# The ends of two feed-forwards: weight splits, residual updates and transposes put in a stated order

## The chip, the cores and the metric

The kernel runs on one core of one Trainium2 chip, in one launch. The metric is the device time of the program in microseconds (us). The engines are named as in the profile: PE is TensorE (PEld its weight loads), DVE is VectorE, ACT is ScalarE, POOL is GpSimd and SP is SyncE, which issues most DMAs. Each engine works through its own list of instructions strictly in the order of that list; an instruction that waits holds up all that stand behind it.

## The reference, cut to what matters

One decoder layer on 512 tokens of width 1024, in float32:

```python
h = x + 0.5 * swiglu(rmsnorm(x, ffn1_norm), ffn1_w_gate, ffn1_w_up, ffn1_w_down)     # width 2816
n = rmsnorm(h, mix_norm)
z = n @ w_in                          # queries, keys, values and gates of two kinds of heads
h = h + concat(attention(z), gla(z)) @ w_out
h = h + 0.5 * swiglu(rmsnorm(h, ffn2_norm), ffn2_w_gate, ffn2_w_up, ffn2_w_down)
gate = sigmoid(rmsnorm(h, ple_gate_norm) @ ple_w_gate)      # 1024 x 1024
emb = rmsnorm(p @ ple_w_proj, ple_norm)                     # 256 -> 1024
h = h + gate * emb

def swiglu(x, w_gate, w_up, w_down):
    return (silu(x @ w_gate) * (x @ w_up)) @ w_down
def rmsnorm(x, g):
    return x * rsqrt(mean(x * x) + 1e-6) * g
```

## The kernel before

**Tiles and products.** The 512 tokens are four tiles of 128. The running sum `h` is four tiles of 128 tokens by 1024 columns. Every large product is made from three PE products: both factors are split into a high part (`hi`, rounded to the PE's float32r) and a low part (`lo`, what is left), and hi·hi, hi·lo and lo·hi are added in one PSUM bank (`mm3`). So each weight tile is loaded by a DMA (`wraw`), cast by ACT to `whi` (line 140) and subtracted by DVE to `wlo` (line 141). `Weights` does this in a fixed order of units: `load` issues the DMA into one of two raw buffers of 1 MB, `split` casts and subtracts into a ring of five slots, and `get(key, ahead)` splits up to a key and some units further.

**The end of a feed-forward.** The last 256 of the 2816 inner columns are handled apart. For each token tile t, `pd(t, q)` makes the last down products for two inner chunks q, into two PSUM banks; `update(t)` adds half of them to `h[t]` (DVE, line 391). The next step needs the norm of `h[t]` turned so that columns lie on partitions: `squares` (ACT, line 307, two halves with their sums), `factor` (a small DVE sum, line 312, and the power -1/2 on POOL, line 299), `scaled` (DVE, line 316), and `turned`, which is `norm_transpose`: eight PE transposes (line 202) into two banks, each bank copied out by an ACT cast to `nhi` (line 292) and a DVE subtraction to `nlo` (line 293). The function `last_tiles` writes out in what order these steps are recorded for the four tiles; `in_order` ties each step behind the last instruction of PE, ACT and DVE recorded so far. A scheduler then puts the instructions of each engine in a list, and may move what isn't tied.

**What follows the two ends.** After the first feed-forward come the products `pe` (p times `ple_w_proj`; four tiles, each 12 PE products and an ACT copy to `eo`), with the last two tiles' transposes after `pe` of tile 1, and then the input projections of the mixing part, first `kvr` (keys, values, ranks). The `pe` products stand in PSUM banks in which the last two `pd` lay, so that they wait for the updates of `h`. After the second feed-forward comes the last gate `pg`: for each half of the columns and each tile, 24 products (`pgt`), a sigmoid on ACT (line 1065), and on DVE the product with `emb` (line 1066) and the sum with `h` (line 1067), then a DMA out. Its weights are four units of 1 MB before.

Of the kernel before, what the change touches and what calls it, by code (L numbers as in the profile page):

```python
# [152 lines left out]
def hymba_kernel(tc, A, out):  # L153
# [50 lines left out]
    def on_pe(f, *args):  # L204

        with tc.issue_after(last_pe[0]):
            return f(*args)
# [76 lines left out]
    for c0 in (0, 512):  # L284
        for k0 in (0, 4):
            W.add_rows("pg", A["ple_w_gate"], k0, 4, c0, 512)

# [35 lines left out]

    def last_tiles(pd, update, gain, nT, name, third=(), fourth=()):

# [12 lines left out]
        def turned(t):  # L338
            norm_transpose(t, sq[t][0], nT, name, (psA, psG))

        in_order((pd, 0, 0), (pd, 1, 0), (pd, 0, 1), (update, 0), (squares, 0), (pd, 1, 1), (update, 1), (factor, 0),
                 (squares, 1), (pd, 2, 0), (pd, 2, 1), *third, (scaled, 0), (update, 2), (factor, 1), (squares, 2),
                 (pd, 3, 0), (pd, 3, 1), (scaled, 1), *fourth, (turned, 0), (update, 3), (factor, 2), (squares, 3),
                 (scaled, 2), (turned, 1), (factor, 3), (scaled, 3))
        return turned
# [211 lines left out]
    with tc.tile_pool(name="ffn1p", bufs=1, reuse_waits="tile") as fp:  # L557
# [4 lines left out]
        turned = []  # L562

        def finish1(pd, update):
            turned.append(last_tiles(pd, update, lambda: gm, nTm, "mx", (), [(keep, 0), (keep, 1), (keep, 2)]))
            keep(3)

        def keep(t):
            nc.sync.dma_start(out=h_d[t], in_=h[t])
# [41 lines left out]
    for t in range(0, NT, 2):  # L611
        eo = mp.tile([P, 8, 256], F32, name=f"eo{t}", tag="e", bufs=2).rearrange("p (t a) c -> p t (a c)", t=2)
        for i in range(2):
# [4 lines left out]
            nc.sync.dma_start(out=emb_d[t + i], in_=eo[:, i])  # L618
            if t + i in (1, 2):
                turned[0](t + i + 1)  # L620

# [376 lines left out]
    with tc.tile_pool(name="ffn2p", bufs=1, reuse_waits="tile") as fp:  # L998
# [38 lines left out]
        nT3 = norm_pair(np_, "pg")  # L1037
        def split_gates():
            W.get(("pg", 0, 0), 0)

        def finish2(pd, update):
            turned[:] = [last_tiles(pd, update, lambda: g3[0], nT3, "pg", [(split_gates,)])]

# [3 lines left out]
    with tc.tile_pool(name="outp", bufs=1, reuse_waits="tile") as op:  # L1047
# [6 lines left out]
        for c0 in (0, 512):  # L1054
            tiles = [W.get(("pg", c0, k)) for k in (0, 2, 4, 6)]
            for t in range(NT):
                if c0 == 0 and t in (1, 2):
                    turned[0](t + 1)
                parts = ((0, 256), (256, 512)) if c0 and t == NT - 1 else ((0, 512),)
                for a, b in parts:  # L1060
                    sl = slice(c0 + a, c0 + b)
                    ps = psA(f"pgt{c0}_{t}_{a}")[:, :b - a]
                    gemm_ts(ps, nT3, t, [(wh[:, :, a:b], wl[:, :, a:b]) for wh, wl in tiles])
                    sg = op.tile([P, 512], F32, name=f"sgm{c0}_{t}_{a}", tag="sgm", bufs=3)[:, :b - a]
# [63 lines left out]
```

## Time and profile before

| | |
|---|---|
| three runs, median (lowest to highest) | 1008.62 us (1008.01 to 1010.85) |
| the profiled execution: its time, and its span from first to last instruction | 1008.22 us, 1006.5 us |
| PE busy | 971.2 us, 96% of the span |
| DVE, ACT, POOL busy | 64%, 39%, 4% |
| mean granted clock of PE | 0.989 of full speed |

The span is what the trace covers; the time of the execution is 1.7 us more. All positions below are microseconds from the start of the span. The first feed-forward ends at about 364 us and the second at about 948 us. In a row of a timeline the first number is the start, the second how long the row's instructions took from the first's start to the last's end, `x16` how many instructions are merged in it, and a bracket at its end says how long the engine stood idle before it and what released it. Matmuls are pipelined: one 128x512 product is shown with 0.39 us, while the next one starts 0.227 us later.

### The profile page before, as it was taken

The page shows a single profiled execution, that of the slowest core. Times are in us where ns is not written, and L with a number is a line of the kernel's source. Part 1 is how long each engine was busy: PE and PEld are TensorE (multiplying, and loading weights), DVE is VectorE, ACT ScalarE, POOL GpSimd, SP SyncE. Part 2 cuts the span into 40 slices and gives each one's busy share as a digit, 9 for nine tenths or more (in the row PEclk, how much of TensorE's full clock was granted, in tenths as well). Part 3 has the DMA queues.
Part 4 walks back from the last instruction along what each step waited for, and adds up shares of the span by engine and source line. Part 5 has one row for each costly group of instructions (what it writes and reads, how often), then busy time and mean ns, then how long its engine had stood idle before and what let it go on. Part 6 is the DMA issues. An engine that isn't in the chain of part 4 may idle for free.

```text
span 1006.5 us, 12373 instructions
## 1 busy us (share of the span) xinstructions
PE 971.2 (96%) x5090; PEld 807.4 (80%) x5090; DVE 645.0 (64%) x811; ACT 394.5 (39%) x569; POOL 43.7 (4%) x55
## 2 busy tenths in 40 slices
PE   5999999999999989998998999999999999999898
PEld 5988888888888879876766789888888888888687
DVE  6567667576675764775766364766677675757652
ACT  5443333333333245585455243333344333332441
POOL 4000000000000010200002010000000000000010
PEclk9999999999999999999998999999999999999999
DMA  8715133141330255220213246142252523303231
GB/s 290 250 47 168 41 126 125 46 167 40 126 105 1 88 186 184 88 85 1 58 50 98 84 163 242 42 168 84 96 205 75 169 83 106 124 1 104 74 126 53
DMA packets 74235, 109.91 MB, mean 109 GB/s; under 512 B 5937, under 2 KB 55234, under 8 KB 74178
## 3 DMA queue, kind: packets, MB, share of 16 engines
q1 hardware_dynamic: 72450, 102.82, 30.4%
q0 software_dynamic: 1728, 6.29, 1.8%
q8 instruction: 40, 0.66, 0.2%
q14 instruction: 17, 0.14, 0.0%
HBM read 100.72 MB, written 8.39 MB: 108 GB/s over the span
## 4 chain that ended last, share of the span: by engine, by line
PE 88%; DVE 6%; ACT 2%; DMA 2%; issue 1%; POOL 0%; SPq 0%; ACTq 0%; POOLq 0%; DVEq 0%
PE pg L199 24%; PE pu L199 24%; PE pd L199 20%; PE pgt L199 5%; PE wo L199 4%; PE aq L199 2%; PE pe L199 1%; PE kvr L199 1%; PE gqk L199 1%; PE gv L199 1%; PE gog L199 1%; DVE mx L724 1%; DMA wraw<-in_w_out_dram 1%; DVE wlo L141 1%; DVE e L722 1%
## 5 line engine op out<-in xcount | busy, mean ns | idle before, releaser
L140 ACT CAST whi<-wraw 128x1024 fp32r<-128x1024 f32 (+1 forms) x126 | 129.9, 1039 | 187.4 <-PE pd L199 136.3
L141 DVE TENSOR_TENSOR wlo<-wraw,whi 128x1024 fp32r<-128x1024 f32 (+1 forms) x124 | 149.9, 1215 | 56.0 <-ACT whi L140 53.7
L199 PE MATMUL pg<-nlo_f,whi 128*128 128x512 f32 (+1 forms) x384 | 143.0, 373 | 0.0
L199 PE MATMUL pg<-nhi_f,whi 128*128 128x512 f32 (+1 forms) x384 | 142.6, 373 | 0.2 <-ACT nhi_f L292 0.2
L199 PE MATMUL pu<-nhi_f,wlo 128*128 128x512 f32 (+1 forms) x384 | 142.6, 372 | 0.0
L199 PE MATMUL pg<-nhi_f,wlo 128*128 128x512 f32 (+1 forms) x384 | 142.6, 372 | 0.0
L199 PE MATMUL pu<-nlo_f,whi 128*128 128x512 f32 (+1 forms) x384 | 142.6, 372 | 0.0
L199 PE MATMUL pu<-nhi_f,whi 128*128 128x512 f32 (+1 forms) x384 | 142.4, 372 | 0.0
L199 PE MATMUL pd<-whi,ahi 128*128 128x512 f32 x312 | 121.4, 389 | 0.0
L199 PE MATMUL pd<-wlo,ahi 128*128 128x512 f32 x312 | 121.4, 389 | 0.0
L199 PE MATMUL pd<-whi,alo 128*128 128x512 f32 x312 | 120.6, 389 | 0.0
L391 DVE SCALAR_TENSOR_TENSOR h<-pd,h 128x512 f32<-128x512 f32 x116 | 76.5, 686 | 29.5 <-PE pd L199 29.5
L199 PEld LDWEIGHTS pg<-nhi_f,whi 128*128 128x128 f32 x384 | 72.3, 189 | 13.2 <-ACT nhi_f L292 0.7
L199 PEld LDWEIGHTS pg<-nlo_f,whi 128*128 128x128 f32 x384 | 72.6, 189 | 12.9 <-DVE nlo_f L293 0.6
L199 PEld LDWEIGHTS pg<-nhi_f,wlo 128*128 128x128 f32 x384 | 72.5, 189 | 12.5
L199 PEld LDWEIGHTS pu<-nhi_f,wlo 128*128 128x128 f32 x384 | 72.3, 188 | 12.5
L199 PEld LDWEIGHTS pu<-nhi_f,whi 128*128 128x128 f32 x384 | 72.2, 188 | 12.5
L199 PEld LDWEIGHTS pu<-nlo_f,whi 128*128 128x128 f32 x384 | 72.4, 188 | 12.3
L140 ACT CAST whi<-draw 128x1024 fp32r<-128x1024 f32 x35 | 36.8, 1053 | 96.9 <-PE pu L199 50.9
L431 DVE TENSOR_TENSOR cb<-pu,sg 128x512 f32<-128x512 f32 x44 | 30.3, 690 | 69.2 <-PE pu L199 69.2
L140 ACT CAST whi<-wpr 128x1024 fp32r<-128x1024 f32 x35 | 36.9, 1053 | 96.2 <-PE pu L199 58.2
L199 PEld LDWEIGHTS pd<-whi,ahi 128*128 128x128 f32 x312 | 58.6, 188 | 12.2
(243 smaller groups left out, 1466.5 us busy)
## 6 DMA issues: line engine op xcount, KB each, us to landing
wraw<-in_ffn_w_gate_dram SPq DMA_DIRECT2D x22, 1024.0 KB, 5.0
wraw<-in_ffn_w_up_dram SPq DMA_DIRECT2D x22, 1024.0 KB, 5.0
wpr<-in_ffn_w_down_dram SPq DMA_DIRECT2D x10, 1024.0 KB, 5.6
draw<-in_ffn_w_down_dram SPq DMA_DIRECT2D x10, 1024.0 KB, 5.2
wraw<-in_w_in_dram SPq DMA_DIRECT2D x8, 1024.0 KB, 4.9
wraw<-in_ple_w_gate_dram SPq DMA_DIRECT2D x4, 1024.0 KB, 4.8
h<-in_x_dram SPq DMA_DIRECT2D x4, 512.0 KB, 7.0
wraw<-in_ffn_w_down_dram SPq DMA_DIRECT2D x4, 512.0 KB, 3.4
```

What stands on the lines that cost most here:

```text
L140: nc.scalar.copy(hi, v)
L141: (nc.gpsimd if u < 2 and i else nc.vector).tensor_tensor(lo, v, hi.bitcast(F32), op=ALU.subtract)
L199: last_pe[0] = nc.tensor.matmul(o, lhsT=l, rhs=r, start=start, stop=stop_, **kw).ins
L391: nc.vector.scalar_tensor_tensor(hs, x, 0.5, hs, ALU.mult, ALU.add)
L431: nc.vector.tensor_mul(cb[:, half].rearrange("p a c -> p (a c)"), pu, sg)
L722: nc.vector.tensor_add(half, sc[:, :, :, :nk], amask[:, 256 - nk:].unsqueeze(1).unsqueeze(1).broadcast_to([P, 2, 2, nk]))
L724: nc.vector.reduce_max(mxt.rearrange("p (g a) -> p g a", g=2)[:, :, 2 * a:2 * a + 2], half, AX.X)
```

## The change

Three things are written anew. First, the order of the steps in `last_tiles`: the common part now ends with the last `pd`, and each feed-forward gives a list of `places` for the rest. Second, the first two of the `pg` weights for the first half of the columns are loaded and split as two units of 512 KB instead of one of 1 MB, the first of them before the last down products, the next two between the steps of the second end; and the first `kvr` unit is split at a stated place of the first end. Third, the last two tiles' transposes: after the first end the code has them behind `pe` of tiles 0 and 1 instead of 1 and 2 (on PE's list they stand behind `pe` of tile 1 in both kernels; new there is that the first twelve products of `kvr` tile 0 follow them, ahead of `pe` of tile 2), and in the gate they stand in the middle of the 24 products of tiles 1 and 2 instead of ahead of them.

```diff
     for c0 in (0, 512):
-        for k0 in (0, 4):
-            W.add_rows("pg", A["ple_w_gate"], k0, 4, c0, 512)
+        for k0, nk in ((0, 2), (2, 2), (4, 4)) if c0 == 0 else ((0, 4), (4, 4)):
+            W.add_rows("pg", A["ple_w_gate"], k0, nk, c0, 512)
...
-    def last_tiles(pd, update, gain, nT, name, third=(), fourth=()):
+    def last_tiles(pd, update, gain, nT, name, places):
...
-        in_order((pd, 0, 0), (pd, 1, 0), (pd, 0, 1), (update, 0), (squares, 0), (pd, 1, 1), (update, 1), (factor, 0),
-                 (squares, 1), (pd, 2, 0), (pd, 2, 1), *third, (scaled, 0), (update, 2), (factor, 1), (squares, 2),
-                 (pd, 3, 0), (pd, 3, 1), (scaled, 1), *fourth, (turned, 0), (update, 3), (factor, 2), (squares, 3),
-                 (scaled, 2), (turned, 1), (factor, 3), (scaled, 3))
+        named = {"pd": pd, "update": update, "squares": squares, "factor": factor, "scaled": scaled, "turned": turned}
+        in_order((pd, 0, 0), (pd, 1, 0), (pd, 0, 1), (update, 0), (squares, 0), (pd, 1, 1), (update, 1), (squares, 1),
+                 (factor, 0), (pd, 2, 0), (pd, 2, 1), (scaled, 0), (factor, 1), (update, 2), (scaled, 1),
+                 (pd, 3, 0), (pd, 3, 1), *((named.get(f, f), *args) for f, *args in places))
         return turned
...
-            turned.append(last_tiles(pd, update, lambda: gm, nTm, "mx", (), [(keep, 0), (keep, 1), (keep, 2)]))
-            keep(3)
+            turned.append(last_tiles(pd, update, lambda: gm, nTm, "mx", [
+                ("update", 3), ("turned", 0), ("squares", 2), ("factor", 2), ("turned", 1), ("squares", 3),
+                (keep, 0), (keep, 1), ("scaled", 2), ("factor", 3), (keep, 2), (lambda: W.get(("kvr", 0, 0), 0),),
+                ("scaled", 3), (keep, 3)]))
...
-            if t + i in (1, 2):
-                turned[0](t + i + 1)
+            if t + i < 2:
+                turned[0](t + i + 2)
...
-        def split_gates():
-            W.get(("pg", 0, 0), 0)
+        def split_gates(k):
+            W.get(("pg", 0, k), 0)

         def finish2(pd, update):
-            turned[:] = [last_tiles(pd, update, lambda: g3[0], nT3, "pg", [(split_gates,)])]
+            split_gates(0)
+            turned[:] = [last_tiles(pd, update, lambda: g3[0], nT3, "pg", [
+                ("squares", 2), ("turned", 0), ("factor", 2), (split_gates, 2), (split_gates, 4), ("turned", 1),
+                ("scaled", 2), ("update", 3), ("squares", 3), ("factor", 3), ("scaled", 3)])]
...
-                if c0 == 0 and t in (1, 2):
-                    turned[0](t + 1)
...
-                    gemm_ts(ps, nT3, t, [(wh[:, :, a:b], wl[:, :, a:b]) for wh, wl in tiles])
+                    wt = [(wh[:, :, a:b], wl[:, :, a:b]) for wh, wl in tiles]
+                    if c0 == 0:
+                        on_pe(gemm_ts, ps, nT3, t, wt[:2], False)
+                        if t in (1, 2):
+                            on_pe(turned[0], t + 1)
+                        on_pe(gemm_ts, ps, nT3, t, wt[2:], True, 4)
+                    else:
+                        gemm_ts(ps, nT3, t, wt)
```

What stands on the engines can differ from what the code's order says, since the scheduler fills in. Three places follow, each as it was and as it is. In the names, the number at the end is the buffer's; `h_92`, `h_93` and `h_94` are tiles 1, 2 and 3 of `h` in the first part.

DVE at the end of the first feed-forward, before: the update of tile 3 is the third step from the end.

```order
L391 SCALAR_TENSOR_TENSOR h_93<-pd_0_2_2606,h_93 128x512
L391 SCALAR_TENSOR_TENSOR h_93<-pd_1_2_2610,h_93 128x512
L312 SCALAR_TENSOR_TENSOR ms_mx_2623<-ss_mx_2603 128x1
L316 SCALAR_TENSOR_TENSOR nrm_mx_2602<-h_92,rs_mx_2625,gain_mix_norm 128x1024
L141 TENSOR_TENSOR wlo_0_2804<-wraw_2800,whi_0_2803 128x544
L141 TENSOR_TENSOR wlo_1_2808<-wraw_2800,whi_1_2807 128x544
L293 TENSOR_TENSOR nlo_mix<-ntr_mx_0_2649,nhi_mix 128x4x128
L293 TENSOR_TENSOR nlo_mix<-ntr_mx_1_2656,nhi_mix 128x4x128
L391 SCALAR_TENSOR_TENSOR h_94<-pd_0_3_2631,h_94 128x512
L391 SCALAR_TENSOR_TENSOR h_94<-pd_1_3_2635,h_94 128x512
```

The same place after:

```order
L312 SCALAR_TENSOR_TENSOR ms_mx_2621<-ss_mx_2599 128x1
L391 SCALAR_TENSOR_TENSOR h_93<-pd_0_2_2606,h_93 128x512
L391 SCALAR_TENSOR_TENSOR h_93<-pd_1_2_2610,h_93 128x512
L316 SCALAR_TENSOR_TENSOR nrm_mx_2598<-h_92,rs_mx_2623,gain_mix_norm 128x1024
L391 SCALAR_TENSOR_TENSOR h_94<-pd_0_3_2628,h_94 128x512
L391 SCALAR_TENSOR_TENSOR h_94<-pd_1_3_2632,h_94 128x512
L293 TENSOR_TENSOR nlo_mix<-ntr_mx_0_2644,nhi_mix 128x4x128
L293 TENSOR_TENSOR nlo_mix<-ntr_mx_1_2651,nhi_mix 128x4x128
```

The update of tile 3 stands directly behind the scaling of tile 1; the two `kvr` weight splits and the first `nlo` copies, which stood ahead of it, stand behind it (the splits now between the small sum and the scaling of tile 3).

DVE at the end of the second feed-forward, before: `nrm_pg_7039` and `nrm_pg_7055` are the scaled tiles 0 and 1, which the first transposes read.

```order
L312 SCALAR_TENSOR_TENSOR ms_pg_7051<-ss_pg_7040 128x1
L141 TENSOR_TENSOR wlo_0_7076<-wraw_7073,whi_0_7075 128x1024
L141 TENSOR_TENSOR wlo_1_7080<-wraw_7073,whi_1_7079 128x1024
L316 SCALAR_TENSOR_TENSOR nrm_pg_7039<-h_0_4388,rs_pg_7053,gain_ple_gate_norm 128x1024
L391 SCALAR_TENSOR_TENSOR h_2_4390<-pd_0_2_7059,h_2_4390 128x512
L391 SCALAR_TENSOR_TENSOR h_2_4390<-pd_1_2_7063,h_2_4390 128x512
L312 SCALAR_TENSOR_TENSOR ms_pg_7086<-ss_pg_7056 128x1
L141 TENSOR_TENSOR wlo_0_7168<-wraw_7165,whi_0_7167 128x1024
L141 TENSOR_TENSOR wlo_1_7172<-wraw_7165,whi_1_7171 128x1024
L316 SCALAR_TENSOR_TENSOR nrm_pg_7055<-h_1_4389,rs_pg_7088,gain_ple_gate_norm 128x1024
```

The same place after, where `nrm_pg_7045` and `nrm_pg_7057` are those two tiles:

```order
L312 SCALAR_TENSOR_TENSOR ms_pg_7061<-ss_pg_7046 128x1
L316 SCALAR_TENSOR_TENSOR nrm_pg_7045<-h_0_4388,rs_pg_7063,gain_ple_gate_norm 128x1024
L312 SCALAR_TENSOR_TENSOR ms_pg_7080<-ss_pg_7058 128x1
L391 SCALAR_TENSOR_TENSOR h_2_4390<-pd_0_2_7065,h_2_4390 128x512
L391 SCALAR_TENSOR_TENSOR h_2_4390<-pd_1_2_7069,h_2_4390 128x512
L316 SCALAR_TENSOR_TENSOR nrm_pg_7057<-h_1_4389,rs_pg_7082,gain_ple_gate_norm 128x1024
L293 TENSOR_TENSOR nlo_pg<-ntr_pg_0_7105,nhi_pg 128x4x128
L293 TENSOR_TENSOR nlo_pg<-ntr_pg_1_7112,nhi_pg 128x4x128
L312 SCALAR_TENSOR_TENSOR ms_pg_7119<-ss_pg_7102 128x1
L141 TENSOR_TENSOR wlo_0_7126<-wraw_7123,whi_0_7125 128x1024
L141 TENSOR_TENSOR wlo_0_7132<-wraw_7129,whi_0_7131 128x1024
L141 TENSOR_TENSOR wlo_1_7136<-wraw_7129,whi_1_7135 128x1024
```

Four weight splits stood between the small sum of tile 0 and the scaling of tile 1. Now none does: one stands far ahead, just before the first addition to `U_0` behind the last product of chunks 16 to 19, and three behind the first `nlo` copies.

PE in the gate, before: `pgt_0_0_7195` and `pgt_1_0` are tiles 0 and 1 of the first half of the columns, `nrm_pg_7090` and `nrm_pg_7129` the scaled tiles 2 and 3.

```order
L199 MATMUL pgt_0_0_7195<-whi_1_7171,nlo_pg 128x512
L202 MATMUL ntr_pg_1_7232<-idn,nrm_pg_7090 128x128 x4
L202 MATMUL ntr_pg_0_7225<-idn,nrm_pg_7090 128x128 x4
L202 MATMUL ntr_pg_1_7276<-idn,nrm_pg_7129 128x128 x4
L199 MATMUL pgt_1_0_7239<-whi_0_7075,nhi_pg 128x512
```

The same tiles after, where `nrm_pg_7101` is the scaled tile 2:

```order
L199 MATMUL pgt_1_0_7227<-wlo_0_7126,nhi_pg 128x512
L199 MATMUL pgt_1_0_7227<-whi_0_7125,nlo_pg 128x512
L202 MATMUL ntr_pg_0_7240<-idn,nrm_pg_7101 128x128 x4
L202 MATMUL ntr_pg_1_7247<-idn,nrm_pg_7101 128x128 x4
L199 MATMUL pgt_1_0_7227<-whi_0_7131,nhi_pg 128x512
```

The gate of tile 1 follows that of tile 0 at once; the transposes of tile 2 stand behind its twelfth product, and those of tile 3 behind the twelfth and the eighteenth of tile 2.

## Rows read from the trace of the kernel before

**Rows 1.** Who waited for whom, PE: total us, times, longest us.

```profile
PE ntr_pg L202 <- ACT whi L140: 3.7, 1, 3.7
PE pe L199 <- DVE h L391: 2.5, 1, 2.5
```

**Rows 2.** Chain that ended last, 350 to 400 us: start, us, what.

```profile
369.14 7.38 PE pe L199 x24
...
378.27 5.46 PE pe L199 x24
383.72 11.98 PE kvr L199 x96
```

**Rows 3.** Timeline of PE, at the two ends and at 575 us.

```profile
364.47 2.16 PE L202 MATMUL ntr_mx<-idn,nrm_mx 128*128 128x128 f32 x16
...
575.03 0.50 PE L199 MATMUL wo<-wlo,nhi_mo 128*128 128x512 f32 x1 [1.69 <-DVE wlo L141]
...
948.94 1.06 PE L202 MATMUL ntr_pg<-idn,nrm_pg 128*128 128x128 f32 x8 [1.04 <-DVE nrm_pg L316]
953.67 1.57 PE L202 MATMUL ntr_pg<-idn,nrm_pg 128*128 128x128 f32 x8 [3.67 <-ACT whi L140]
...
969.28 0.50 PE L199 MATMUL pgt<-whi,nhi_pg 128*128 128x512 f32 x1 [0.25 <-ACT sgm L1065]
```

**Rows 4.** Timeline of DVE, end of the first feed-forward.

```profile
362.06 1.28 DVE L391 SCALAR_TENSOR_TENSOR h<-pd,h 128x512 f32<-128x512 f32 x2
...
364.13 1.29 DVE L316 SCALAR_TENSOR_TENSOR nrm_mx<-h,rs_mx,gain_mix_norm 128x1024 f32<-128x1024 f32 x1 [0.73 <-POOL rs_mx L299]
365.34 1.35 DVE L141 TENSOR_TENSOR wlo<-wraw,whi 128x544 fp32r<-128x544 f32 x2
366.61 1.28 DVE L293 TENSOR_TENSOR nlo_mix<-ntr_mx,nhi_mix 128x512 fp32r<-128x512 f32 x2
367.81 1.28 DVE L391 SCALAR_TENSOR_TENSOR h<-pd,h 128x512 f32<-128x512 f32 x2
```

**Rows 5.** Timeline of ACT, end of the first feed-forward.

```profile
362.77 0.63 ACT L307 ACTIVATE nrm_mx<-h 128x512 f32<-128x512 f32 x1 [1.84 <-DVE h L391]
...
365.27 1.07 ACT L292 CAST nhi_mix<-ntr_mx 128x512 fp32r<-128x512 f32 x2
```

**Rows 6.** Stretches: us; busy of PE, PEld, DVE, ACT, POOL; PE clock; DMA.

```profile
371.00:372.00 1.00, 1.00 (x4) 0.80 (x3) 1.00 (x3) 0.00 (x0) 0.00 (x0) 0.50 1.05 428
...
576.00:577.00 1.00, 1.00 (x6) 0.79 (x5) 1.00 (x2) 0.00 (x0) 0.00 (x0) 1.00 0.00 0
```

**Rows 7.** Timeline of DVE, end of the second feed-forward.

```profile
945.24 2.36 DVE L141 TENSOR_TENSOR wlo<-wraw,whi 128x1024 fp32r<-128x1024 f32 x2 [1.77 <-ACT whi L140]
947.52 1.28 DVE L316 SCALAR_TENSOR_TENSOR nrm_pg<-h,rs_pg,gain_ple_gate_norm 128x1024 f32<-128x1024 f32 x1
...
949.98 2.35 DVE L141 TENSOR_TENSOR wlo<-wraw,whi 128x1024 fp32r<-128x1024 f32 x2
952.25 1.28 DVE L316 SCALAR_TENSOR_TENSOR nrm_pg<-h,rs_pg,gain_ple_gate_norm 128x1024 f32<-128x1024 f32 x1
```

**Rows 8.** Chain that ended last, 945 to 975 us.

```profile
955.25 6.55 PE pgt L199 x24
```

**Rows 9.** Timeline of POOL, end of the second feed-forward.

```profile
943.62 0.55 POOL L299 TENSOR_TENSOR rs_pg<-ms_pg,nhalf 128x1 f32<-128x1 f32 x1 [180.74 <-DVE ms_pg L312]
950.21 1.40 POOL L299 TENSOR_TENSOR rs_pg<-ms_pg,nhalf 128x1 f32<-128x1 f32 x1 [6.04 <-DVE ms_pg L312]
```

**Rows 10.** Timelines of SP, ACT and DVE, 915 to 927 us.

```profile
917.65 5.17 SPq L104 DMA_DIRECT2D wraw<-in_ple_w_gate_dram  x2
...
920.11 1.05 ACT L140 CAST whi<-wraw 128x1024 fp32r<-128x1024 f32 x1 [3.75 <-PE pd L199]
...
925.28 0.69 DVE L412 TENSOR_TENSOR U<-U,pd 128x512 f32<-128x512 f32 x1 [1.66 <-PE pd L199]
```

**Rows 11.** Weight loads (`wraw`) between 905 and 980 us: time to landing.

```profile
DMA to landing us min/median/max: 3.4/4.8/5.8
```

## The prediction, made before the result was known

> **What bounds the kernel now.** I read the busy shares first: PE works 96% of the span, so what can be won is PE's idle time and the time in which it runs at the lower clock. The list of PE's waits comes next. It names two places which the change touches: 2.5 us before the first `pe`, put down to DVE's update of `h`, and 3.7 us before a transpose in the gate, put down to an ACT cast [rows 1]; PE's own timeline adds 1.04 us before the transposes of tile 0 [rows 3]. Then I looked at what the engine named did just before.
>
> At the first end PE's 16 transposes run from 364.47 to 366.63 [rows 3], and `pe` starts at 369.14 [rows 2]. DVE shows why: the update of tile 3 ends at 369.09, since the scaling of tile 1, two `kvr` splits (1.35 us) and two `nlo` copies (1.28 us) stand ahead of it [rows 4], although its products were done when the transposes began. The wait has a second price. In the stretch 371 to 372 the clock is 0.50, the level of 1.2 GHz [rows 6], and the 24 products of `pe` tiles 0 and 1 take 7.38 us where the next 24 take 5.46 [rows 2].
>
> At the second end the scaling of tile 0 starts at 947.52 behind two splits (2.36 us), and that of tile 1 at 952.25 behind two more (2.35 us) [rows 7]. PE's transposes start at 948.94 and 953.67 [rows 3], each right after the scaling that it reads. So the 3.7 us are DVE's too; the ACT cast merely ended at the same moment. The first 24 gate products then take 6.55 us [rows 8] instead of 5.46.
>
> **The change part by part. First end.** The update of tile 3 now follows the scaling of tile 1. The small sum of tile 1 stands ahead of the update of tile 2, so that update runs about 0.15 us later than 362.06 and ends at 363.4. The power of tile 1 was there 0.88 us after its sum's start (0.15 sum, 0.73 wait [rows 4]), now at 363.0, hidden by the update. The scaling runs 363.4 to 364.7, 0.7 earlier than 364.13. The last `pd` ends where the transposes begin, so the update of tile 3 runs from about 364.7 to 366.0. The banks of `pe` are free 0.6 us before PE has finished its transposes at 366.63. The wait of 2.51 goes, and with it the slow clock, 7.38 − 5.46 = 1.92. Together 4.43.
>
> What is late next? PE would end the 24 `pe` at 372.1 and transposes of tile 2 at 373.1; tile 3 must be scaled by then. ACT casts the first `nhi` pair 365.3 to 366.3 (0.8 us after the transposes start as now, 1.07 long [rows 3, 5]), then squares of tile 2 (two halves of 0.63) to 367.5, the second `nhi` pair to 368.6, squares of tile 3 to 369.8, two `kvr` casts to 371.1. DVE follows: `nlo` pair of tile 0 366.0 to 367.2, `nlo` of tile 1 to 369.3, scaling of tile 2 to 370.6, sum of tile 3 to 370.7, two `kvr` splits to 372.0, scaling of tile 3 then to 373.3, if the power of 0.88 us is hidden under the splits. Beside a split POOL's power took 1.40 us, without one 0.55 [rows 9], so it may come 0.85 later, and the scaling ends between 373.3 and 373.7. PE waits 0.2 to 0.7 us there; I take 0.5. The trace agrees with the Trainium skill, "SBUF — State Buffer", section "SBUF: two separate sides": whichever of DVE and GpSimd takes the shared port pair first has it for a whole instruction. By that rule the upper end counts, and the gain would be 0.2 us less.
>
> Nothing else at this end costs PE time. The first 12 of the 96 `kvr` products (11.98 us in all [rows 2], so 1.5) only change places with `pe` of tiles 2 and 3, and cover the copy of `eo`, which ACT now does behind `nhi` of tile 2. The second load of the queries' weights leaves SP when `kvr`'s split frees its buffer, 372 instead of 366.7, but its cast comes after 382, and loads landed within 5.8 us [rows 11]. The four writes of `h` stand ahead of it on SP and are ready by 366. First end: 4.43 − 0.5 = 3.9. Bounds: 2.5 with the clock still falling and 0.5 more in stalls, 4.4 with no new wait.
>
> **Second end.** The first split moves far ahead, in front of an addition to `U` on DVE. The cast of the unit before it starts at 920.11, when the fourth of seven groups of products has freed a ring slot [rows 10]; the fifth group, 12 products of 0.227, frees the next near 922.8. Its load leaves SP at 917.65 [rows 10] and is half as long as before. ACT stands idle from 921.2, so the cast ends near 923.9 and the split near 925.1, ahead of the addition at 925.28. It costs nothing; behind it some 8 us of additions wait, with 3 us to spare before the last `pd` need their factors.
>
> With no split ahead, tile 0's power is there at 944.2 (943.62 + 0.55 [rows 9]) and its scaling done at 945.5, before the last `pd` end at 947.9 (948.94 − 1.04). The update of tile 2 runs to 946.8, the scaling of tile 1 to 948.0. PE turns both tiles without a gap from 947.9, in 2.16 us as at the first end [rows 3], to 950.05. The first gate product needs `nlo` of tile 0. ACT's squares of tile 2 are done at 948.1, its `nhi` pair runs 948.7 to 949.7, DVE's pair ends at 950.5, its first half at 949.9: no wait. Six products (1.36 us) use the split made early. The seventh and eighth need the second one: ACT casts it 949.7 to 950.75 (1.05 [rows 10]), DVE splits it by 952.0, while PE asks at 951.4, so PE waits 0.6. The third and fourth follow at 1.2 us each (half of 2.35 [rows 7]) and PE takes 1.36 for six products, so these are in time. The 24 products end at about 956.0 where they now end at 961.8 (955.25 + 6.55 [rows 8]), 5.8 earlier.
>
> From there tile 1's 24 products need its `nlo` (955.3) and free bank; the transposes of tile 2 come after twelve, at 958.7, and its scaling ends at 956.7. Those of tile 3 are asked for at about 965.1. Its scaling waits for a chain: the sigmoid of tile 0 (956.1 to 956.7), a cast for the next half, two squares (to 959.3), sum, power, `nlo` of tile 2: done near 961.9, three microseconds early. The 0.25 us for the sigmoid [rows 3] goes: the third tile's product takes the bank that tile 2's transposes left. Against this I set 0.3 us for `nlo` of tile 3, which now stands behind two products with `emb` on DVE. Second end: 5.8. Bounds: 3.5, if two bank waits (0.6 covered by transposes plus 0.25 each) and another 0.6 in the weights return; 6.5, if there is no wait at all (13.9 us from 947.9 to 961.8 against 2.16 + 5.46, plus 0.25).
>
> The one load more costs SP half a microsecond in an idle time. The mixing part between keeps its order; its waits hang on PE's own earlier results and move with it.
>
> **The sum.** 1008.22 (span 1006.5 and 1.7 around it) − 3.9 − 5.8 = 998.5. The profiled execution lies 0.4 below the median 1008.62, so I predict 998.9 for the median.
>
> **Rivals.** (a) *The gate gives a part back.* After the scaling of tile 1 DVE has `nlo`, three splits, `nlo` and a scaling without a pause, and ACT its casts in between; if one comes late, PE works in pieces. For it: DVE is the last engine at every step there. Against: PE's demand is slower than DVE's supply. Price: a pause as long as that before `pe` would bring a slow spell like its own, 1.9 us [rows 2]: 1000.8. That short waits alone bring the lower clock the rows don't show: after 1.69 us of idleness at 573 [rows 3] the stretch 576 to 577 has clock 1.00, 2.4 GHz [rows 6]. The Trainium skill says otherwise, in "TensorE: Matmul & The Clock Gate", section "A second HAM failure mode": frequent small idle times between groups of matmuls can make the clock oscillate. By that rule the price of (a) would fall due although no wait is long.
>
> (b) *Only the gate counts.* The mixing part has stretches where PE waits for ACT and DVE; if their work didn't start earlier by the 3.9 us, the first end would be given back: 1008.6 − 5.8 = 1002.8. Against: what DVE and ACT do there starts from products of PE, and nothing is bound to a fixed time.
>
> (c) *The change doesn't act.* If `pe` and the transposes wait for something else than the named steps, all stays: 1008.6. Against: three starts that follow an end on DVE within 0.25 us.
>
> (d) *Slower.* ACT's list has the cast of the next half's first weights between the first sigmoid and the squares of tile 3. This load leaves SP only when the second split frees its buffer, at 952.0. While it is out, ACT stands, and behind it the squares, the scaling and the transposes of tile 3, amid tile 2's products on PE. It is due at 956.7 (median 4.8 [rows 11]), and there are 3 us in hand; from 960 on every microsecond counts in full, and from a landing at 970 the kernel is slower than before. With a landing at 973, 1012. Against: no load here took over 5.8 us.
>
> **How the numbers follow.** Chances: forecast 0.64, (a) 0.17, (b) 0.10, (c) 0.06, (d) 0.03. The forecast's own range, from the bounds of both ends, is 996.5 (no new wait, and a little from the mixing part) to 1000.5; with (a) and (b) inside, 996.5 to 1003.0 leaves out (c), (d) and little else. A difference of 0.3%, 3 us, is about what can be told from none. Faster by more: forecast, (a), (b), with 0.91 together; within it (c), 0.06; slower (d), 0.03.
>
> **What would show it.** Right: `pe` follows the transposes at the first end without a wait on DVE, and its first 24 products take 5.5 us at clock 1.00; the update of tile 3 ends before 366.6; in the gate the transposes follow the last `pd` directly, the first 24 products end about 5.8 us earlier relative to them; the stretch between the two ends is as long as before. Wrong: a new wait of over 1 us on PE before the transposes of tile 3 at either end, a clock below 1 in the gate, a longer last stretch of `pd` at the second end (the early split holding up DVE), or a mixing part that is longer by what the first end gave.

## The result, and the profile after

The changed kernel takes 997.49 us (median, 996.72 to 998.50) beside 1008.32 us (1006.18 to 1010.85) for the kernel before, measured together: 0.9892 of it, with a 95% interval of 0.9867 to 0.9917. A second measurement gave 997.16 us beside 1006.83 us, a ratio of 0.9904 (0.9888 to 0.9920). The forecast was 998.9 us with the range 996.5 to 1003.0, and faster.

The profiled execution takes 998.5 us with a span of 996.7 us. PE's list of waits comes first (who waited for whom, total us, times, longest us), since it answers to [rows 1]:

```profile
PE ntr_f L202 <- DVE nrm_f L316: 8.1, 1, 8.1
...
PE ntr_mx L202 <- DVE nrm_mx L316: 0.4, 1, 0.4
...
PE pgt L199 <- DVE nlo_pg L293: 0.2, 1, 0.2
```

Both lines of [rows 1] are gone. The 8.1 us for `nrm_f` is not of this change (8.2 before). What is new are 0.4 us at the first end and 0.2 us in the gate.

The timeline of PE at the first end, beside the first row of [rows 3]:

```profile
365.38 1.91 PE L202 MATMUL ntr_mx<-idn,nrm_mx 128*128 128x128 f32 x16
367.05 0.48 PE L199 MATMUL pe<-whi,pTwhi 128*128 128x512 f32 x1
...
372.59 1.03 PE L202 MATMUL ntr_mx<-idn,nrm_mx 128*128 128x128 f32 x8
373.99 1.06 PE L202 MATMUL ntr_mx<-idn,nrm_mx 128*128 128x128 f32 x8 [0.37 <-DVE nrm_mx L316]
...
392.74 0.39 PE L199 MATMUL aq<-whi,nhi_mix 128*128 128x512 f32 x1
```

`pe` follows the transposes at once and its first 24 products end at 372.59, 5.5 us after their start. The stretch 371 to 372, which had the clock 0.50 in [rows 6], now has 1.00 (the number behind the five engines):

```profile
371.00:372.00 1.00, 1.00 (x6) 0.84 (x5) 1.00 (x4) 0.60 (x2) 0.47 (x1) 1.00 0.00 0
```

The timeline of DVE shows why, beside [rows 4]:

```profile
364.24 1.27 DVE L316 SCALAR_TENSOR_TENSOR nrm_mx<-h,rs_mx,gain_mix_norm 128x1024 f32<-128x1024 f32 x1
365.43 1.28 DVE L391 SCALAR_TENSOR_TENSOR h<-pd,h 128x512 f32<-128x512 f32 x2
...
371.30 1.35 DVE L141 TENSOR_TENSOR wlo<-wraw,whi 128x544 fp32r<-128x544 f32 x2
372.57 1.28 DVE L316 SCALAR_TENSOR_TENSOR nrm_mx<-h,rs_mx,gain_mix_norm 128x1024 f32<-128x1024 f32 x1
```

The update of tile 3 starts with the transposes and is done before they end. The scaling of tile 3 (372.57) is the last to come, behind the two `kvr` splits: that is the new wait of 0.37 us.

In the gate PE's timeline reads, beside the `ntr_pg` and `pgt` rows of [rows 3]:

```profile
943.54 1.91 PE L202 MATMUL ntr_pg<-idn,nrm_pg 128*128 128x128 f32 x16
945.53 0.50 PE L199 MATMUL pgt<-whi,nhi_pg 128*128 128x512 f32 x1
...
947.03 0.39 PE L199 MATMUL pgt<-whi,nhi_pg 128*128 128x512 f32 x1
947.50 0.50 PE L199 MATMUL pgt<-wlo,nhi_pg 128*128 128x512 f32 x1
...
954.22 1.03 PE L202 MATMUL ntr_pg<-idn,nrm_pg 128*128 128x128 f32 x8
...
964.56 0.50 PE L199 MATMUL pgt<-whi,nhi_pg 128*128 128x512 f32 x1 [0.19 <-DVE nlo_pg L293]
```

The 1.04 and 3.67 us of idleness are gone, and the 0.25 us for the sigmoid. Between 945.53 and 964.56 PE runs 72 gate products and the last transposes, and the list of waits names none there. One small delay is hidden in the rows: the eighth product starts 0.47 us after the seventh where 0.227 is the pace, so 0.24 us late, right behind the split of the second piece (946.22 to 947.46). The chain that ended last shows what is late now (start, us, what):

```profile
946.22 1.24 DVE wlo L141
...
947.48 4.92 DMA wraw<-in_ple_w_gate_dram
...
952.48 1.06 ACT whi L140
...
953.56 1.23 DVE wlo L141
...
955.10 0.55 POOL rs_pg L299
...
956.17 5.62 DMA emb<-emb_d
...
961.89 0.70 DVE sgm L1076
...
964.56 27.80 PE pgt L199 x144
```

A load, of the next half, starts when the split of the second piece frees its buffer; its cast and split hold up the small sum and the power of tile 3. Behind that power POOL issues the loads of `emb`, DVE waits for one of them before its product with `emb`, and the low part of tile 3 stands behind that product. It is late by 0.19 us (0.39 in r2_after_again; in r4_gate_only PE doesn't wait there at all).

I divided each profile into four stages: from the start to the first `ntr_mx`, from there to the first `aq` (the first end), on to the end of the last `pd` (the middle), and to the end of the span (the last stage). The two profiles differ by +0.91, 27.36 − 31.07 = −3.71, 550.95 − 552.37 = −1.42 and 53.01 − 58.59 = −5.58 us, together −9.8. The forecast had 0, −3.9, 0 and −5.8.

### The profile page after: what moved, and what is told of

Read it like the earlier page. It is cut to its first block, busy times and chain, and to the rows that moved or that the text cites. A ratio compares the mean times of both kernels' runs of the same rounds, so it can differ in the third digit from the quotient of the medians.

```text
span 996.7 us, 12375 instructions
## 1 busy us (share of the span) xinstructions
PE 967.9 (97%) x5090; PEld 805.1 (81%) x5090; DVE 646.0 (65%) x811; ACT 394.5 (40%) x569; POOL 44.7 (4%) x55
## 4 chain that ended last, share of the span: by engine, by line
PE 87%; DVE 6%; DMA 2%; ACT 2%; issue 1%; POOL 0%; SPq 0%; ACTq 0%; DVEq 0%; POOLq 0%
PE pg L199 24%; PE pu L199 24%; PE pd L199 21%; PE wo L199 4%; PE pgt L199 3%; PE aq L199 2%; PE kvr L199 1%; PE gv L199 1%; PE gqk L199 1%; DVE wlo L141 1%; DVE mx L726 1%; DMA wraw<-in_w_out_dram 1%; DVE e L724 1%; PE ntr_f L202 1%; DMA h<-in_x_dram 1%
## 5 line engine op out<-in xcount | busy, mean ns | idle before, releaser
L391 DVE SCALAR_TENSOR_TENSOR h<-pd,h 128x512 f32<-128x512 f32 x116 | 76.5, 685 | 29.5 <-PE pd L199 29.5
L199 PEld LDWEIGHTS pd<-whi,alo 128*128 128x128 f32 x312 | 58.6, 188 | 12.2
```

Of the source, the lines that this page charges most:

```text
L199: last_pe[0] = nc.tensor.matmul(o, lhsT=l, rhs=r, start=start, stop=stop_, **kw).ins
L391: nc.vector.scalar_tensor_tensor(hs, x, 0.5, hs, ALU.mult, ALU.add)
```

## What the experiments asked

My theory was the prediction's: each end gives what its waits and the low clock behind them cost, and the two add up. The rivals: one end is paid back later; at each end only one of the moves matters; and, for the middle, that its −1.42 us belong to the new order and not to chance. This table holds all thirteen profiles, in us; the labels that aren't yet explained are those of the experiments below. The last column is PE's wait before the `pt` transposes near 505 us, and whether the clock fell to 0.50 behind it.

| kernel | start | first end | middle | last stage | span | wait before `pt` |
|---|---|---|---|---|---|---|
| before | 364.47 | 31.07 | 552.37 | 58.59 | 1006.5 | 1.99, fell |
| r1_before_again | 365.33 | 29.48 | 551.76 | 58.63 | 1005.2 | 1.58 |
| v3_before_third | 365.45 | 29.45 | 551.81 | 58.69 | 1005.4 | 1.62 |
| r3_first_end_only | 364.73 | 27.35 | 553.26 | 58.66 | 1004.0 | 2.44, fell |
| u1_update_only | 364.71 | 28.87 | 551.65 | 58.57 | 1003.8 | 1.66 |
| v2_kv_splits_late | 364.66 | 28.56 | 551.91 | 58.67 | 1003.8 | 1.51 |
| r4_gate_only | 364.30 | 31.08 | 552.62 | 52.90 | 1000.9 | 2.42, fell |
| after | 365.38 | 27.36 | 550.95 | 53.01 | 996.7 | 1.57 |
| r2_after_again | 364.43 | 27.44 | 550.16 | 53.27 | 995.3 | 1.80 |
| u2_turns_ahead | 364.32 | 27.44 | 549.99 | 53.45 | 995.2 | 1.41 |
| u3_no_early_split | 364.63 | 27.44 | 552.75 | 61.28 | 1006.1 | 2.01, fell |
| v1_third_buffer | 364.99 | 27.36 | 553.69 | 54.96 | 1001.0 | 2.40, fell |
| u4_more_early | 364.76 | 27.32 | 550.12 | 52.50 | 994.7 | 1.62 |

## Experiments on the two ends and the middle

**The two kernels again.** No edit.

> The kernel before, unchanged, profiled once more, to see how far the stages vary from one execution to the next. Theory A (the middle is shorter in the changed kernel because the stretches of granted clock 0.50 fall differently by chance): the stretch of the middle, from the first aq product to the end of the last pd product, differs by about 1 us or more from the 552.20 us of the first profile, and the stretches at 0.50 stand at other places than 466, 507 and 544. Theory B (the order of the first end sets what happens behind it): 552.2 us within 0.3, with the same stretches. In both the first end, from the first ntr_mx transpose to the first aq product, is 31.2 us with its wait of 2.5 us for h, and the last stage, from the last pd to the end of the span, 58.6 us.

> The kernel before, unchanged, profiled a third time. The wait of 2.51 us for h is there; the question is only whether a stretch at 0.50 follows it. Of three profiles with this order at the first end two had it and one not. Theory A (it falls by chance, by how the run lies in time): transposes to aq either 31.1 or 29.5 us. The wait before pt near 505 us, if 1.8 us or less, is not followed by a stretch at 0.50, and if 2.0 us or more, it is.

> The changed kernel, unchanged, profiled and timed once more: ratio 0.989 to before. First end 27.5 us from the first ntr_mx transpose to the first aq product, last stage 53.2 us. Theory A (chance in the clock's stretches): the middle is anything from 550 to 553.5 us. Theory B (it belongs to the order): 550.7 us within 0.3, and no stretch at 0.50 near 505 us.

Of the kernel before I now have four profiles with the old first end (r4_gate_only has it too). The row on `pe` shows the same wait in all of them; here it is from r1_before_again, with the clock behind it, beside the first row of [rows 6]:

```profile
370.00 0.50 PE L199 MATMUL pe<-whi,pTwhi 128*128 128x512 f32 x1 [2.51 <-DVE h L391]
```

```profile
371.00:372.00 1.00, 1.00 (x6) 0.78 (x6) 1.00 (x2) 0.73 (x2) 0.28 (x1) 1.00 1.09 424
```

In r4_gate_only the same wait is followed by 0.50:

```profile
371.00:372.00 1.00, 1.00 (x4) 0.73 (x3) 1.00 (x3) 0.00 (x0) 0.00 (x0) 0.50 1.01 416
```

So the same idle time of 2.51 us brought the lower clock twice and twice not: it did where the transposes started at 364.30 and 364.47, and not at 365.33 and 365.45. The first end takes 31.1 us in the one case and 29.5 in the other. The 31.2 us that I expected of r1_before_again were wrong, and its middle differs from the first one by 0.6 us, between the two theories; theory A of v3_before_third holds. The middle of r2_after_again, 550.16 us, is what its theory A allows and theory B doesn't. (The expectations count from an `aq` that the chain of work places 0.16 us later.) The Trainium skill, "TensorE: Matmul & The Clock Gate", Part 1, says that the clock gate's watch runs by itself and doesn't begin with the kernel; these four profiles agree, since the same work and the same wait came out both ways.

**Only the first end.** The order of `last_tiles` in the first feed-forward, the place of the `kvr` split and that of the last two tiles' transposes (not shown here) are new, the gate is as before:

```diff
-            turned.append(last_tiles(pd, update, lambda: gm, nTm, "mx", (), [(keep, 0), (keep, 1), (keep, 2)]))
-            keep(3)
+            turned.append(last_tiles_new(pd, update, lambda: gm, nTm, "mx", [
+                ("update", 3), ("turned", 0), ("squares", 2), ("factor", 2), ("turned", 1), ("squares", 3),
+                (keep, 0), (keep, 1), ("scaled", 2), ("factor", 3), (keep, 2), (lambda: W.get(("kvr", 0, 0), 0),),
+                ("scaled", 3), (keep, 3)]))
```

> Only the first feed-forward's end has the new order; the gate and the second end are as before. My theory (the two ends add up, first end 3.7 to 3.9 us by its wait of 2.51 us and the slow clock behind it): transposes to aq 27.5 us, last stage 58.6 us, a time of about 1004.6 us beside 1008.3 of before, ratio 0.9963. Rival (only the gate counts, the first end is paid back before aq): transposes to aq 31 us, ratio 1.000. A middle that is shorter by 1.4 us because of the new first end would show here as well: ratio 0.9950.

1004.41 us, ratio 0.9971 (0.9961 to 0.9981), that is 1.9 to 3.9 us of 1006.83: the rival that gives nothing falls. The profile has 27.35 us from transposes to `aq`, as expected. The size, 2.9 us in the middle of its interval, lies between the 2.1 us that the new end saves where the clock would not have fallen and the 3.7 us where it would. The middle is 553.26 us, longer than in the kernel before and not shorter, and the ratio of 0.9950 that a shorter middle would have given lies outside the interval.

**Only the gate.** The reverse: units, second end and gate as in the changed kernel, the first end as before.

> Only the second end and the gate are changed (the first half's weights loaded in three pieces, split at stated places, the last two transposes amid the products); the first end is as before. My theory (the two ends add up): transposes to aq 31.2 us, last stage 53.2 us instead of 58.6, a time of about 1002.9 us, ratio 0.9946. Rival (the gate gives part back): last stage 55 us or more, ratio 0.9965 or more. If the middle is shorter by the new first end, it is 552.2 us here; if the clock's stretches fall by chance, anything from 550 to 553.5.

1001.74 us, ratio 0.9945 (0.9926 to 0.9963), 3.7 to 7.5 us. The last stage is 52.90 us, 5.7 less than before. The products of the two ratios, 0.9971 times 0.9945, make 0.9916, inside both intervals of the whole change (0.9867 to 0.9917, 0.9888 to 0.9920): nothing speaks against the two ends adding up. It lies at the upper edge of both, so a further microsecond that neither half gives isn't ruled out.

**The middle.** From the first `aq` to the last `pd`, PE's products and transposes are in the same order in all thirteen profiles, by the names of their tiles, and yet the middles run from 549.99 to 553.69 us. Among the eight without a fall of the clock in the last column, the four with the new first end lie lower (549.99 to 550.95 us against 551.65 to 551.91), among the five with a fall, the three with the new first end lie higher (552.75 to 553.69 against 552.37 and 552.62). So no direction can be read, and the −1.42 of the first pair is not shown to be part of the change. One cause can be read. PE's row before `pt` and the stretch around it, in after:

```profile
503.36 1.09 PE L202 MATMUL pt<-idn,e 128*128 128x128 f32 x8 [1.57 <-ACT pb L753]
```

```profile
500.00:512.00 12.00, 10.43 (x170) 8.03 (x170) 9.48 (x12) 6.63 (x10) 0.00 (x0) 1.00 0.24 83
```

and in r3_first_end_only:

```profile
502.94 1.09 PE L202 MATMUL pt<-idn,e 128*128 128x128 f32 x8 [2.44 <-ACT pb L776]
```

```profile
500.00:512.00 12.00, 9.56 (x130) 7.72 (x122) 8.58 (x11) 6.63 (x10) 0.00 (x0) 0.86 0.16 60
```

The mean clock of the twelve microseconds is 1.00 in the one and 0.86 in the other. In all thirteen profiles the five waits of 1.99 to 2.44 us there were followed by 0.50, the eight of 1.41 to 1.80 us were not. Why this wait for ACT varies stays open. A second spell, behind a wait of 3.85 us for `kdT` at 463 us, differs in length; after has a mean clock of 0.79 over 458 to 474, r2_after_again 0.89:

```profile
458.00:474.00 16.00, 11.83 (x126) 9.55 (x126) 5.89 (x11) 9.75 (x28) 0.00 (x0) 0.79 0.00 1
```

```profile
458.00:474.00 16.00, 12.13 (x145) 10.13 (x146) 6.36 (x10) 10.18 (x29) 0.00 (x0) 0.89 0.01 1
```

**The halves of the first end.** The update alone, then the splits alone, each in a copy of `last_tiles` that only the first end uses; u1 moves `(update, 3)` ahead of the kept blocks and the transposes of tile 0, v2 states a place for the splits:

```diff
-                 (pd, 3, 0), (pd, 3, 1), (scaled, 1), *fourth, (turned, 0), (update, 3), (factor, 2), (squares, 3),
+                 (pd, 3, 0), (pd, 3, 1), (scaled, 1), (update, 3), *fourth, (turned, 0), (factor, 2), (squares, 3),
```

```diff
-                 (scaled, 2), (turned, 1), (factor, 3), (scaled, 3))
+                 (scaled, 2), (turned, 1), (factor, 3), (W.get, ("kvr", 0, 0), 0),
+                 (scaled, 3))
```

> The kernel before, with one thing moved: the last update of h stands behind the scaling of tile 1, ahead of the blocks of h that are kept and of the transposes of tile 0. The splits of the key and value weights stay ahead of the low parts of tiles 2 and 3 on VectorE, the rest is as before. My theory (PE waited 2.51 us because the update stood late on VectorE, and the clock fell because PE waited): the wait of pe for h goes, the granted clock stays at 1.00 behind it, transposes to aq 27.0 to 28.5 us, ratio about 0.9963. Rival (the place of the weight splits matters as much): a wait of 1.5 us or more for the low parts of tile 2 or 3 takes its place, transposes to aq 29.5 us or more, ratio 0.998 or more.

> The kernel before, with one thing moved at the first end: the two splits of the key and value weights stand directly ahead of the scaling of tile 3 (their place in the changed kernel), the update of tile 3 stays behind the low parts of tile 0. The other half of what u1_update_only leaves out. If each piece of work ahead of the update on VectorE counts by its length, the wait for h is 2.51 - 1.27 = 1.24 us, and the later wait before the transposes of tile 3 is 0 to 0.4 us; transposes to aq 28.1 to 28.7 us. Rival (the update must come ahead of the low parts, the splits' place is free): the wait stays at 2.5 us, 29.4 us or more. On the clock: if a wait of 1.24 us is short enough not to be followed by a stretch at 0.50, there is none near 370.

u1: 1005.08 us, 0.9977 (0.9966 to 0.9989). v2: 1005.50 us, 0.9977 (0.9963 to 0.9992). PE's timeline of u1, and under it the row of v2:

```profile
372.49 1.04 PE L202 MATMUL ntr_mx<-idn,nrm_mx 128*128 128x128 f32 x8
374.83 1.06 PE L202 MATMUL ntr_mx<-idn,nrm_mx 128*128 128x128 f32 x8 [1.30 <-DVE nrm_mx L316]
```

```profile
368.45 0.50 PE L199 MATMUL pe<-whi,pTwhi 128*128 128x512 f32 x1 [1.63 <-DVE h L415]
```

In u1 the wait of 2.51 us goes, and half of it comes back as 1.30 us before the transposes of tile 3: the splits still stand ahead of all that is scaled later. My expectation that the update alone brings nearly all is wrong, and the rival nearer. In v2 the wait shrinks by 0.88 instead of 1.27 us, because without the splits DVE waits 0.30 us for the casts that the low parts read. By stage, and against the 29.45 us of the old end without a fall of the clock, u1 saves 0.6, v2 0.9 and both together 2.1 us, each from one profile; by time the three ratios, 0.9977, 0.9977 and 0.9971, can't be told apart. Neither alone leaves DVE in time. The clock didn't fall in either, behind 1.30 or 1.63 us.

## Experiments in the gate

**Transposes ahead of the products.** The changed kernel, with the transposes of tiles 2 and 3 where they were:

```diff
+                if c0 == 0 and t in (1, 2):
+                    turned[0](t + 1)
...
-                    if c0 == 0:
-                        on_pe(gemm_ts, ps, nT3, t, wt[:2], False)
-                        if t in (1, 2):
-                            on_pe(turned[0], t + 1)
-                        on_pe(gemm_ts, ps, nT3, t, wt[2:], True, 4)
```

> The changed kernel, with the transposes of tiles 2 and 3 again ahead of the first products of the gate for tiles 1 and 2, instead of amid them (between the pieces of weights). Theory 1 (the place amid the products is what lets PE run through while tile 2 is scaled): PE waits about 1 us for the scaling of tile 2 and up to 0.6 us for the low part of tile 3, the last stage is 54 to 54.8 us instead of 53.2. Theory 2 (the early splits bring the gain alone, the place of the transposes is free): 53.2 us within 0.2.

999.35 us, 0.9910 (0.9891 to 0.9930), not to be told from the changed kernel's 0.9904. PE's timeline has one wait:

```profile
950.32 1.06 PE L202 MATMUL ntr_pg<-idn,nrm_pg 128*128 128x128 f32 x8 [0.60 <-DVE nrm_pg L316]
```

It is less than I expected, and in exchange the wait for `nlo_pg` (0.19 us in after, 0.39 in r2) is gone. The last stage is 53.45 us, 0.2 to 0.5 more than in the three profiles of the whole new gate (52.90, 53.01 and 53.27): theory 2, nearly. Putting the transposes amid the products is worth a few tenths at most, hardly more than these three differ among themselves.

**No early split.**

```diff
-            split_gates(0)
...
-                ("squares", 2), ("turned", 0), ("factor", 2), (split_gates, 2), (split_gates, 4), ("turned", 1),
+                ("squares", 2), ("turned", 0), ("factor", 2), (split_gates, 0), (split_gates, 2), (split_gates, 4), ("turned", 1),
```

> The changed kernel, with the split of the gate's first two blocks of weights not ahead of the last pd products but with the other splits, behind the factor of tile 2: four splits of 1.17 us then stand on VectorE between the low part of tile 0 and that of tile 1. Theory 1 (the early split takes work out of the stretch that VectorE is late in): PE waits 1 to 2 us more before the first gate products or the transposes of tile 1, the last stage is 54.2 to 55.2 us. Theory 2 (VectorE has slack there): 53.2 to 53.4 us. If the wait brings the granted clock down to 0.50, as the waits of 3.67 and 1.04 us did in the gate of before, up to 1.9 us come on top.

1006.41 us, 0.9990 (0.9979 to 1.0001): nearly the whole gain of the change is lost by this one step, 8.3 us in the last stage and far beyond both theories. PE's timeline and the chain:

```profile
947.36 0.50 PE L199 MATMUL pgt<-whi,nhi_pg 128*128 128x512 f32 x1 [0.80 <-ACT whi L140]
948.62 0.50 PE L199 MATMUL pgt<-wlo,nhi_pg 128*128 128x512 f32 x1 [0.76 <-DVE wlo L141]
...
954.62 0.80 PE L199 MATMUL pgt<-whi,nhi_pg 128*128 128x512 f32 x1 [3.23 <-ACT whi L140]
955.88 0.80 PE L199 MATMUL pgt<-wlo,nhi_pg 128*128 128x512 f32 x1 [0.46 <-DVE wlo L141]
```

```profile
947.34 1.24 DVE wlo L141
...
948.60 4.85 DMA wraw<-in_ple_w_gate_dram
...
954.60 1.24 DVE wlo L141
...
955.88 8.06 PE pgt L199 x23
```

```profile
957.00:958.00 1.00, 1.00 (x4) 0.81 (x3) 1.00 (x2) 0.98 (x2) 0.00 (x0) 0.50 0.02 8
```

The load of the third piece leaves at 948.60, when the split of the first is over, and 23 products then take 8.06 us at 0.50 for the most part. Two buffers hold three pieces: the early split gave the third its buffer 27 us sooner. Before, there were only two units for the two buffers, and both were loaded from 917.65 on [rows 10]; the load came to depend on a split only when three pieces had to share two buffers. In after SP issues three loads from 913.43 on, the third 7.5 us behind the first, right after the early split (919.70 to 920.93 on DVE):

```profile
913.43 7.89 SPq L104 DMA_DIRECT2D wraw<-in_ple_w_gate_dram  x3
```

```profile
919.70 1.23 DVE L141 TENSOR_TENSOR wlo<-wraw,whi 128x1024 fp32r<-128x1024 f32 x1 [0.30 <-ACT whi L140]
921.07 0.69 DVE L412 TENSOR_TENSOR U<-U,pd 128x512 f32<-128x512 f32 x1
```

**No early split, but a third buffer.** To part the load from the engines' work, the kernel of u3 with one more edit:

```diff
-        raw_t = self.rawp.tile([P, 2048], F32, name=f"wraw{u}", tag="wraw")
+        if keys[0] == ("pg", 0, 4):
+            raw_t = self.raw2(f"wraw{u}")
+        else:
+            raw_t = self.rawp.tile([P, 2048], F32, name=f"wraw{u}", tag="wraw")
```

> The kernel of u3_no_early_split (no early split), but the third piece of the gate's weights is loaded into a buffer of its own, one that has long been free, so that its load needn't wait until the split of the first piece has freed one of the two buffers. Theory L (the early split matters because it lets the load of the third piece start): the waits of 3.23 and 0.46 us before the thirteenth gate products and the stretch at 0.50 behind them go, what is left are the 0.80 and 0.76 us before the first products and at most 1 us for the later splits; last stage 54.5 to 56 us instead of 61.3. Theory D (the early split matters because it takes 1.2 us of VectorE's work and 1.05 us of ScalarE's out of the stretch): the waits stay, last stage 60 us or more.

1000.64 us, 0.9925 (0.9900 to 0.9950), last stage 54.96 us; the load of the third piece now leaves at 902.42. PE's waits for weights in the gate (beside 0.6 us for `nlo_pg`):

```profile
PE pgt L202 <- ACT whi L143: 0.8, 1, 0.8
PE pgt L202 <- DVE wlo L144: 0.8, 1, 0.8
```

Theory L. Of the 8.3 us that the early split is worth, 61.28 − 54.96 = 6.3 are the load, with its wait and the clock that falls behind it, and 54.96 − 53.01 = 2.0 the work on ACT and DVE. Beside the 58.6 us of before, the 54.96 show something else: with all its weights loaded in time the new order gives 3.6 of the 5.6 us without any early split.

**More of it early.** The second piece is split early too, and the `kvr` splits come behind the scaling of tile 3:

```diff
             split_gates(0)
+            split_gates(2)
...
-                (keep, 0), (keep, 1), ("scaled", 2), ("factor", 3), (keep, 2), (lambda: W.get(("kvr", 0, 0), 0),),
-                ("scaled", 3), (keep, 3)]))
+                (keep, 0), (keep, 1), ("scaled", 2), ("factor", 3), (keep, 2), ("scaled", 3),
+                (lambda: W.get(("kvr", 0, 0), 0),), (keep, 3)]))
```

> The changed kernel, with the second piece of the gate's weights split early as well, and with the splits of the key and value weights behind the scaling of tile 3 in the first end. My theory (the wait of 0.37 us for nrm_mx and that of 0.19 us at the gate's last tile are what is left): 0.2 to 0.8 us less than the changed kernel, ratio to before 0.9885. Rival (the kv weights are then late): PE waits for the splits at the first kvr products, 0.5 to 1 us more than the changed kernel, ratio 0.990.

998.02 us, 0.9905 (0.9888 to 0.9922): by time the same as the changed kernel. By stage the gate has no wait left and takes 52.50 us, 0.4 to 0.8 less; the first end stays at 27.32, since PE then waits 0.17 us for a copy of `eo` instead of 0.37. A gain of this size can't be told here, and no version beats the changed kernel beyond doubt.

## Why the prediction was right, and where it was not

**First end.** The steps came as worked out: no wait for `h`, full clock, the update over by 366.7 (in a profile that lies 0.9 us later there), a new wait of 0.37 us for 0.5, and −3.71 for −3.9. The Trainium skill's rule on the shared port, "SBUF — State Buffer", section "SBUF: two separate sides", has no price here: beside the `kvr` splits POOL's power took 0.90 us instead of 0.55, and the scaling followed the splits without a gap. The power came 0.35 and not 0.85 us later, beside a split of 0.72 us where [rows 9] had splits of 1.2, and was hidden behind the second one. What fails is the term "and with it the slow clock, 7.38 − 5.46 = 1.92". The slow clock was in the profile that I read, but two of the four profiles with that wait don't have it; and where it came it cost 1.6 us (31.07 against 29.48), not 1.92. Over many executions the first end alone gave 2.9 us (1.9 to 3.9), with the 3.9 of the prediction at the edge.

**Second end.** That the wait of 3.67 us was DVE's, and the ACT cast named with it only ended at the same moment, is borne out: r1_before_again and v3_before_third have the same wait and put it down to DVE's scaling. In the changed kernel the transposes follow the last `pd`, the 0.6 us of waiting for the second split shrank to 0.24, and 0.19 us for `nlo` of tile 3 came instead of 0.3. The last stage is 5.58 us shorter for 5.8. About 0.4 us is lost behind the last product: from there to the end it is 4.34 us (964.56 + 27.80 to 996.7) where it was 3.97 (1002.53 to 1006.5). All seven profiles with the new gate have 4.3 to 4.4 us there and all six with the old one 3.9 to 4.0; why stays open, and the prediction had nothing for it.

**The early split** was put at nothing, and that is what it costs: DVE adds to `U` directly behind it, at 921.07. But I had only looked at what it does to DVE. That it lets the third piece be loaded, without which 6.3 us would be lost again, is a step that the prediction didn't have. It said of these pieces only that they "are in time".

**The middle.** Forecast unchanged, and no change is shown, within its own spread of 3.7 us. The 1.42 us less of the first pair are no more than that spread.

**The sum.** The 9.7 us came as 9.8 in the first pair and as 9.7 by the second ratio, but such closeness is in part luck: the first pair holds +0.9 and −1.4 us that no experiment ties to the change, and a profile of before that happened to have the slow clock. The two ends measured by themselves give 2.9 and 5.5 us, 8.4 together. The range was also not what the prediction says it follows from: the bounds of both ends, 6.0 and 10.9 us together, lead from 1008.6 to 997.7 and 1002.6, and not to 996.5 and 1000.5. The 1.2 us "from the mixing part" at the lower end rest on no row, and without them the median of 997.49 would lie 0.2 us below the range.

**Rivals.** (a) falls: no wait in the gate is listed with more than 0.19 us, and the clock stays at 1.00 through it:

```profile
943.00:975.00 32.00, 31.64 (x154) 25.68 (x153) 23.36 (x30) 16.63 (x26) 4.20 (x6) 1.00 0.45 165
```

The Trainium skill's rule on small idle times ("TensorE: Matmul & The Clock Gate", section "A second HAM failure mode") is not put to the test by so little; in u2_turns_ahead a wait of 0.60 us in the gate left the last stage at 53.45 us. (b) falls by the first end's own 0.9971. (c) falls by the starts of `pe` and `ntr_pg`. (d): the load that it fears left at 947.48 instead of 952.0, landed after 4.92 us, and did reach the chain, by way of the loads of `emb`, at a price of 0.19 us.

## What to carry to other kernels

Ask of a piece of work that is moved early not only what it delays or spares on its engine, but which buffer it frees and what is loaded into that: here three quarters of a step's worth was the load behind it. Ask too whether the new pieces are what made that load late. Price the low clock behind a short wait from several executions, since one profile shows it as certain or as absent. And compare kernels stage by stage before a difference of one microsecond is put down to an edit: a stage in which PE's order never changed moved by up to 3.7 us.

## What the runs showed that I had not expected

The same wait of 2.51 us was followed by the granted clock 0.50 in two of four profiles. At another place waits of 1.99 us and more did in five of five, and 1.80 us and less in none of eight; in the old gate 1.04 and 3.67 us close together did in all six profiles that have it. One wait too many costs twice: in the run without the early split 3.23 and 0.46 us of waiting were followed by 23 products in 8.06 us, where 24 take 5.46 at full clock.
